# Two pads of 32 bytes between the tile pools of a two-layer decoder trunk

## The chip, the cores and the metric

The kernel runs on one core of one Trainium2 chip. The metric is the device time of one execution in microseconds. The kernel before takes 1494.91 us as the median of three runs (1493.44 to 1496.66). The core has a tensor engine (TensorE, PE in the profile, with PEld for its weight loads), a vector engine (VectorE, DVE), a scalar engine (ScalarE, ACT), GpSimd (POOL) and SyncE (SP), which here issues all DMAs. Two memories matter: SBUF, with 128 partitions in which every tile has a start byte, and PSUM, into which matmuls write.

## The reference

A trunk of two layers over 512 tokens of width 1024, in float32. Each layer is a token mixer, a layer norm, a squared-ReLU MLP of width 4096 with a layer norm, and a gate with a per-layer input p:

```python
for i in range(DEPTH):
    mix = ssd_mixer(x, ...) if i % 2 == 0 else hgrn2_mixer(x, ...)
    h = layer_norm(DEEPNORM_ALPHA * x + mix, ln_g[i, 0], ln_b[i, 0])
    h = layer_norm(DEEPNORM_ALPHA * h + sq_relu_mlp(h, mlp_w1[i], mlp_w2[i]), ln_g[i, 1], ln_b[i, 1])
    x = h + jax.nn.sigmoid(h @ ple_w_gate[i]) * (p[i] @ ple_w_proj[i])
```

Layer 0 mixes with Mamba-2's SSD (an input projection to 5152 columns, a causal convolution, 32 heads in chunks of 128 tokens, an output projection from 2048), layer 1 with HGRN2 (a projection to 4096 columns, 8 heads, an output projection from 1024).

## The kernel before

All projections are made with numbers split in two. A weight unit of 128 x 1024 is loaded by SyncE into a tile `raw`, ScalarE casts it to float32r as the high part `whi` (L104), and VectorE subtracts to get the low part `wlo` (L106). Activations are split in the same way into tiles of the pool `b8`, through the class `Split`, whose `h` and `l` return slices of the high and the low part. A product is then three matmuls that accumulate into one bank of PSUM, high by high, high by low and low by high, which the helper `mm3` issues:

```python
def mm3(out, sh, sl, mh, ml, start, stop):
    nc.tensor.matmul(out, sh, mh, start=start, stop=False)   # L110
    nc.tensor.matmul(out, sh, ml, start=False, stop=False)   # L111
    nc.tensor.matmul(out, sl, mh, start=False, stop=stop)    # L112
```

The first operand (`sh`, `sl`) is loaded into the array as weights, a slice of 128 x 128; the second (`mh`, `ml`) is streamed, 512 or 256 columns at a time. In the profile a matmul reads `out<-streamed,weights`. Every matmul has a weight load of its own, which starts with the matmul before it.

There are three uses of `mm3`:

- `project` and the Strassen products load `whi` and `wlo` as weights and stream the activations: `pj<-b,whi`, `pj<-b,whi`, `pj<-b,wlo` for L110, L111 and L112.
- `out_part`, the gate and the HGRN values load the activations and stream the weights: `pj<-whi,b`, `pj<-wlo,b`, `pj<-whi,b`. In the gate `py<-whi,a` and its like use the split p, `p_s`, in two tiles of the pool `w4`.
- `strassen` makes most pairs of hidden tiles of the MLP with seven products of blocks in place of eight. Four of its blocks are sums; three of these lie in tiles `S`, high part and low part side by side, the fourth in `b8`. `pj<-S,whi`, `pj<-S,whi` and `pj<-S,wlo` are its products with an `S` block, with 256 columns streamed.

The MLP goes over eight groups of four hidden tiles in the order of the list `ORDER`; the first three pairs of hidden tiles are plain products. Outside of HGRN, where TensorE's order is written out, the framework's scheduler orders each engine's work; it gives the weight units a lead.

Memory in SBUF is taken pool by pool, in the order in which the pools are opened: `consts`, `raws`, `whip`, `wlop`, `b8`, `accp`, `w4`, `sm`, and at last one pool per phase for temporaries (`S`, `z`, `xs`, `cv` and others). A pool's tiles have fixed slots one behind the other, and nearly all of these slots are multiples of 512 bytes long. So a pool's start byte fixes the offset of all its tiles, and all slices that the projections' matmuls take start at multiples of 512 bytes from a tile's start.

Of the kernel before, what the change touches and what calls it, by code (L numbers as in the profile page):

```python
# [15 lines left out]
P = 128  # L16
# [13 lines left out]
# the first pairs of hidden tiles are plain products, the others Strassen's  # L30
PLAIN = 3
ORDER = [(w[0], int(w[1])) for w in "h0 b0 h1 o0 h2 o1 h3 o2 h4 o3 h5 o4 h6 o5 h7 o6 o7".split()]
# HGRN: the projections in their order, and how much of them goes between the steps of two heads
# [9 lines left out]
def trunk(ctx: ExitStack, tc, a):  # L43
# [4 lines left out]
    whip = pool("whip", 5)  # L48
    wlop = pool("wlop", 5)
    b8 = pool("b8", 9)  # L50
# [24 lines left out]
    def begin(name):  # L75
        """the pool of temporaries of a phase, in place of the phase before's"""
        if phase:
            phase[1].__exit__(None, None, None)
            phase.clear()
        phase.append(tc.tile_pool(name=name, bufs=1, reuse_waits="tile"))  # L80
        phase.append(phase[0].__enter__())
        phase.reverse()
        phase.append(bufs[name])
# [13 lines left out]
    # ---------------------------------------------------------------- weights  # L97
# [16 lines left out]
    class Split:  # L114
        """[128, n, 512] as high and low parts, in slots of four rows each."""
# [11 lines left out]
    def project(src, xs, ps, m=P, tok=slice(0, T)):  # L127
        """ps[m, tok] = W[:, tile].T @ x.T for a weight unit of eight row tiles."""
        hi, lo = src
        for k in range(8):  # L130
            c = slice(k * m, (k + 1) * m)
            mm3(ps[:m, tok], hi[:, c], lo[:, c], xs.h(k, tok), xs.l(k, tok), k == 0, k == 7)

    # ---------------------------------------------------------------- constants
# [35 lines left out]
    # ---------------------------------------------------------------- layer norm and friends  # L170
# [7 lines left out]
    def layer_norm(c, gb):  # L178
        """acc[:, c] = LN(acc[:, c])"""
        src = acc[:, c, :]  # L180
        st = mk(sm, [P, 2, 6], "lnst")
        for h in range(2):
            nc.vector.bn_stats(st[:, h, :], src[:, h * 512 : (h + 1) * 512])
        mv = mk(sm, [P, 2], "lnmv")
        nc.vector.bn_aggr(mv, st.rearrange("p a b -> p (a b)"))
        sd = mk(sm, [P, 1], "lnsd")
        nc.scalar.activation(sd, mv[:, 1:2], AF.Sqrt, bias=eps)
        rs = mk(sm, [P, 1], "lnrs")
        nc.vector.reciprocal(rs, sd)
        nc.vector.scalar_tensor_tensor(src, src, mv[:, 0:1], gb[0], ALU.subtract, ALU.mult)  # L190
        nc.vector.scalar_tensor_tensor(src, src, rs, gb[1], ALU.mult, ALU.add)

    def transpose_split(src, dst, c, keep=None):
        """dst[:, k, chunk c] = src[tokens, k-th 128 features].T, split; unsplit in keep"""
        sl = slice(c * P, (c + 1) * P)
        for q in range(2):
            pt = bank(pst, "pt")
            for j in range(4):
                k = 4 * q + j
                nc.tensor.transpose(pt[:, j * P : (j + 1) * P], src[:, k * P : (k + 1) * P], ident)  # L200
            v = pt.rearrange("p (j t) -> p j t", j=4)
            h = dst.hi[q][:, :, sl]
            nc.scalar.copy(h, v)
            nc.vector.tensor_sub(dst.lo[q][:, :, sl], v, f32(h))
            if keep is not None:
                nc.scalar.copy(keep[q][:, :, sl], v)

    def out_part(units, n, xs, c, h, first, scale):
        """acc[:, c, half h] += x[:, chunk c].T @ W over n row tiles, each token's row by scale if given;
        acc holds alpha * residual (or the residual, if first)"""  # L210
        sl = slice(c * P, (c + 1) * P)
        ps = bank(psj, "pj")
        for k in range(n):
            hi, lo = units[k // 2]
            ks = slice((k % 2) * 512, (k % 2 + 1) * 512)
            mm3(ps, xs.h(k, sl), xs.l(k, sl), hi[:, ks], lo[:, ks], k == 0, k == n - 1)
        d = acc[:, c, h * 512 : (h + 1) * 512]
        if scale is not None:
            nc.vector.scalar_tensor_tensor(d, ps, scale[:, c : c + 1], d, ALU.mult, ALU.add)
        elif first:  # L220
            nc.vector.scalar_tensor_tensor(d, d, ALPHA, ps, ALU.mult, ALU.add)
        else:
            nc.vector.tensor_add(d, ps, d)  # L223

    def out_project(w, xs, first, after=None, scale=None):
        """w: the four units of four row tiles, by halves of the columns; after(c): what follows the last of chunk c"""
        if after is not None:
            units = [unit(w[i]) for i in range(4)]
            for c in range(NCH):
                for h in range(2):  # L230
                    out_part(units[2 * h : 2 * h + 2], 4, xs, c, h, first, scale)
                after(c)
        else:
            for h in range(2):
                units = [unit(w[2 * h + i]) for i in range(2)]
                for c in range(NCH):
                    out_part(units, 4, xs, c, h, first, scale)

    def norm(i):
        """the norm's result, transposed and split, and what makes its chunk c"""  # L240
        gb = ln_params(i)
        h_s = Split(8)
        keep = [mk(b8, [P, 4, T], "b8") for _ in range(2)] if i % 2 == 0 else None

        def chunk(c):
            layer_norm(c, gb)
            transpose_split(acc[:, c, :], h_s, c, keep)

        return h_s, chunk, keep

    # Winograd's form of Strassen's product: seven products of blocks for eight. The blocks of h.T are
    # [token half][k half], those of the weights [k half][output tile].
    def block_sums(h_s, ht):
        """the four plain and four summed blocks of h.T, as (high, low) of a row tile k"""
# [28 lines left out]
    def weight_sums(src1, src2):  # L283
        """the seven blocks of two weight units: B11, B21, B22, T1, T2, T3, B21 - T2, as (high, low, column)"""
# [24 lines left out]
    def strassen(blocks, src1, src2, z):  # L309
        """z[:, m] = W[:, tile m].T @ h.T for two weight units"""  # L310
# [34 lines left out]
    def mlp_and_gate(layer, h_s, ht, last):  # L345
        """acc holds the normed h. Returns the next x, transposed and split, with x in acc."""
# [40 lines left out]
        # gate  # L387
# [45 lines left out]
    # ---------------------------------------------------------------- layer 0: SSD  # L433
    # time steps
# [36 lines left out]
    # dt * exp(cs_last - cs)  # L471
# [6 lines left out]
    def dt_tail():  # L478
        # token-major copies: [128 tokens, chunk, head]
# [10 lines left out]
    def conv_silu(ps, i, out):  # L490
        """out = silu(causal conv of ps + bias), channel tile i of the convolved ones"""
        cv = tmp("cv", [P, T])
        nc.scalar.activation(cv, ps, AF.Identity, scale=convw[:, i, 3:4], bias=convb[:, i : i + 1])
        for k in range(3):
            d = 3 - k
            nc.vector.scalar_tensor_tensor(cv[:, d:], ps[:, : T - d], convw[:, i, k : k + 1], cv[:, d:], ALU.mult, ALU.add)
        nc.scalar.activation(out, cv, AF.Silu)
# [44 lines left out]
    def core(j, xs, sz, y, toks, btok, cbm, cm):  # L542
# [3 lines left out]
        # token-major x * dt and x * dt * decay to the chunk's end  # L546
# [11 lines left out]
        # chunk states and their scan  # L558
# [13 lines left out]
        # masked decays times C B  # L572
# [9 lines left out]
        # decay from the chunk's start, on channels  # L582
# [33 lines left out]
    def rms_group(ss):  # L616
        """1 / rms of each token of the group: [128 tokens, chunk]"""
# [52 lines left out]
    # ---------------------------------------------------------------- layer 1: HGRN2  # L670
# [6 lines left out]
    # lower bounds: softmax over the one layer, cumulated, less its first row  # L677
# [11 lines left out]
    # The tensor engine's order is fixed here: the projections of the heads to come fill the waits of a head's scores.  # L689
    def vg(i):  # L690
        """values and output gates of heads 2i and 2i + 1, by tokens: [128, chunk, 256]"""
# [80 lines left out]
    def hcore(h, s, i, hl):  # L772
# [12 lines left out]
        def column_sums(f, n):  # L785
            """the sums over the partitions, on each of them"""
# [8 lines left out]
        # the scores of a token with itself and of an odd one with the token before it  # L795
# [63 lines left out]
        # states  # L859
# [23 lines left out]
        # norm and output gate  # L883
# [5 lines left out]
        ri = mk(sm, [P, NCH], "hri")  # L889
# [51 lines left out]
def _tiles_m(w):  # L941
    """[K, M] -> [M/128, 128, K/128 * 128]: one unit per 128 output channels"""
# [4 lines left out]
def _tiles_g(w):  # L947
    """[K, 1024] -> [K/128, 128, 1024]: per four row tiles, two units for each half of the columns"""
# [5 lines left out]
def _tiles_h(w):  # L954
    """[K, 1024] -> [2 * K/256, 128, 2 * 512]: by halves of the columns, two row tiles each"""
# [5 lines left out]
def _tiles_q(w):  # L961
    """[1024, 1024] -> [4, 2, 128, 4 * 256]: by quarters of the columns, four row tiles each"""
# [4 lines left out]
def _cols(v):  # L967
    """[n * 128] -> [128, n]"""
# [3 lines left out]
def _rows(v):  # L972
    """[K, T] -> [128, K/128, T]"""
# [70 lines left out]
```

## Time and profile before

| | |
|---|---|
| median of three runs | 1494.91 us |
| span of the profiled execution | 1492.3 us (the runs' whole times are listed above; for the profiled one the page gives its span) |
| TensorE busy | 1479.3 us, 8848 matmuls |
| weight loads busy (beside the matmuls) | 1280.9 us, 8848 |
| VectorE busy | 1096.4 us, 1786 instructions |
| ScalarE busy | 711.2 us, 968 instructions |
| GpSimd busy | 0.9 us, 8 instructions |
| DMA | 150.07 MB, 101 GB/s on average |
| time in matmuls of L110, L111, L112 on the chain that ended last | 29%, 28%, 28% of the span |

How to read it: matmuls are pipelined, so the duration of one says little of what it costs in a row of them; the distance between the starts of two matmuls in the timeline does. A group's row gives line, engine, operation, tiles, shape and count, then busy us and mean ns of one, then the engine's idle time ahead of it with what ended it.

### The profile page before, as it was taken

The page shows a single profiled execution, that of the slowest core. Times are in us where ns is not written, and L with a number is a line of the kernel's source. Part 1 is how long each engine was busy: PE and PEld are TensorE (multiplying, and loading weights), DVE is VectorE, ACT ScalarE, POOL GpSimd, SP SyncE. Part 2 cuts the span into 40 slices and gives each one's busy share as a digit, 9 for nine tenths or more (in the row PEclk, how much of TensorE's full clock was granted, in tenths as well). Part 3 has the DMA queues.
Part 4 walks back from the last instruction along what each step waited for, and adds up shares of the span by engine and source line. Part 5 has one row for each costly group of instructions (what it writes and reads, how often), then busy time and mean ns, then how long its engine had stood idle before and what let it go on. Part 6 is the DMA issues. An engine that isn't in the chain of part 4 may idle for free.

```text
span 1492.3 us, 21964 instructions
## 1 busy us (share of the span) xinstructions
PE 1479.3 (99%) x8848; PEld 1280.9 (86%) x8848; DVE 1096.4 (73%) x1786; ACT 711.2 (48%) x968; POOL 0.9 (0%) x8
## 2 busy tenths in 40 slices
PE   8999999999999999999999999999999999999998
PEld 5888888888989999888778998989898999998887
DVE  6998677797886777776844767769787777777673
ACT  5777455563564434444334453543364444444342
POOL 0000000000000000000000000000000000000000
PEclk9999999999999999999999999999999999999999
DMA  6433223332233323244223222222123333324322
GB/s 237 169 102 111 98 100 113 100 113 85 71 99 99 113 82 103 88 139 129 94 71 114 86 66 77 70 72 72 57 72 99 114 113 100 110 79 150 115 71 71
DMA packets 41621, 150.07 MB, mean 101 GB/s; under 512 B 4624, under 2 KB 5136, under 8 KB 41392
## 3 DMA queue, kind: packets, MB, share of 16 engines
q1 hardware_dynamic: 41520, 148.67, 30.1%
q8 instruction: 70, 1.15, 0.3%
q14 instruction: 31, 0.25, 0.1%
HBM read 146.49 MB, written 2.16 MB: 100 GB/s over the span
## 4 chain that ended last, share of the span: by engine, by line
PE 97%; DMA 1%; DVE 1%; ACT 1%; issue 0%; SPq 0%; ACTq 0%; DVEq 0%
PE pj L110 29%; PE pj L111 28%; PE pj L112 28%; PE py L782 1%; PE py L591 1%; PE pt L200 1%; PE pm L561 1%; PE py L596 1%; PE py L792 1%; PE py L827 1%; DMA raw<-in_wg 1%; DVE wlo L106 0%; PE pt L549 0%; PE py L880 0%; PE py L112 0%; PE py L110 0%
## 5 line engine op out<-in xcount | busy, mean ns | idle before, releaser
L110 PE MATMUL pj<-whi,b 128*128 128x512 f32 (+1 forms) x1096 | 401.5, 367 | 0.5 <-ACT z L414 0.5
L111 PE MATMUL pj<-wlo,b 128*128 128x512 f32 (+1 forms) x1096 | 399.3, 364 | 0.5 <-DVE wlo L106 0.5
L112 PE MATMUL pj<-whi,b 128*128 128x512 f32 (+1 forms) x1096 | 399.8, 365 | 0.0
L110 PE MATMUL pj<-b,whi 128*128 128x256 f32 (+1 forms) x1024 | 348.0, 340 | 2.1 <-ACT whi L104 2.1
L112 PE MATMUL pj<-b,wlo 128*128 128x256 f32 (+1 forms) x1024 | 344.2, 336 | 0.0
L111 PE MATMUL pj<-b,whi 128*128 128x256 f32 (+1 forms) x1024 | 343.7, 336 | 0.0
L104 ACT CAST whi<-raw 128x1024 fp32r<-128x1024 f32 x192 | 201.4, 1050 | 229.6 <-PE pj L111 133.4
L106 DVE TENSOR_TENSOR wlo<-raw,whi 128x1024 fp32r<-128x1024 f32 x192 | 233.9, 1220 | 64.4 <-ACT whi L104 62.4
L111 PEld LDWEIGHTS pj<-wlo,b 128*128 128x128 f32 x1096 | 206.8, 189 | 32.2 <-DVE wlo L106 1.0
L110 PEld LDWEIGHTS pj<-whi,b 128*128 128x128 f32 x1096 | 206.6, 189 | 32.3 <-ACT z L414 0.7
L112 PEld LDWEIGHTS pj<-whi,b 128*128 128x128 f32 x1096 | 206.7, 189 | 31.7 <-issue 0.2
L110 PEld LDWEIGHTS pj<-b,whi 128*128 128x128 f32 x1024 | 194.5, 190 | 22.0 <-ACT whi L104 4.7
L112 PEld LDWEIGHTS pj<-b,wlo 128*128 128x128 f32 x1024 | 194.4, 190 | 20.3 <-DVE b L150 1.7
L111 PEld LDWEIGHTS pj<-b,whi 128*128 128x128 f32 x1024 | 194.6, 190 | 18.3 <-issue 1.9
L293 ACT CAST whi<-raw 128x1024 fp32r<-128x1024 f32 (+1 forms) x52 | 43.4, 835 | 136.2 <-PE pj L112 110.4
L223 DVE TENSOR_TENSOR acc<-pj,acc 128x512 f32<-128x512 f32 x120 | 81.6, 686 | 35.0 <-PE pj L112 34.5
L110 PE MATMUL pj<-S,whi 128*128 128x256 f32 x312 | 87.4, 280 | 0.0
L111 PE MATMUL pj<-S,whi 128*128 128x256 f32 x312 | 87.0, 279 | 0.0
L112 PE MATMUL pj<-S,wlo 128*128 128x256 f32 x312 | 87.0, 279 | 0.0
L295 DVE TENSOR_TENSOR wlo<-raw,whi 128x1024 fp32r<-128x1024 f32 (+1 forms) x52 | 49.7, 957 | 35.0 <-ACT whi L293 35.0
L293 ACT CAST whi<-a 128x1024 fp32r<-128x1024 f32 x26 | 27.3, 1050 | 94.8 <-PE pj L111 45.5
L110 PEld LDWEIGHTS pj<-S,whi 128*128 128x128 f32 x312 | 58.7, 188 | 0.0
(217 smaller groups left out, 1810.6 us busy)
## 6 DMA issues: line engine op xcount, KB each, us to landing
raw<-in_w SPq DMA_DIRECT2D x128, 512.0 KB, 3.4
raw<-in_wssd SPq DMA_DIRECT2D x40, 512.0 KB, 3.4
a<-csd SPq DMA_DIRECT2D x16, 512.0 KB, 4.0
raw<-in_wso SPq DMA_DIRECT2D x16, 512.0 KB, 3.3
raw<-in_wg SPq DMA_DIRECT2D x16, 512.0 KB, 3.8
raw<-in_whvg SPq DMA_DIRECT2D x16, 512.0 KB, 3.3
raw<-in_whq SPq DMA_DIRECT2D x16, 512.0 KB, 3.3
raw<-in_who SPq DMA_DIRECT2D x8, 512.0 KB, 3.3
```

The source lines that it names most:

```text
L104: nc.scalar.copy(hi[:, :n], raw[:, :n])
L106: nc.vector.tensor_sub(lo[:, :n], raw[:, :n], f32(hi[:, :n]))
L110: nc.tensor.matmul(out, sh, mh, start=start, stop=False)
L111: nc.tensor.matmul(out, sh, ml, start=False, stop=False)
L112: nc.tensor.matmul(out, sl, mh, start=False, stop=stop)
L200: nc.tensor.transpose(pt[:, j * P : (j + 1) * P], src[:, k * P : (k + 1) * P], ident)
L223: nc.vector.tensor_add(d, ps, d)
L293: nc.scalar.copy(hi[:, :n], f)
L295: nc.vector.tensor_sub(lo[:, :n], f, f32(hi[:, :n]))
L561: nc.tensor.matmul(pst_[:, c * P : (c + 1) * P], btok[:, c, :], xw[:, c].rearrange("p h q -> p (h q)"), start=True, stop=True)
L591: nc.tensor.matmul(yd[64 * r : 64 * r + 64, sl], xdt[:, 2 * c + r, :], m[:, r, sl], start=True, stop=True)
L596: nc.tensor.matmul(yo[:, c * P : (c + 1) * P], pv[:, c - 1].rearrange("p h q -> p (h q)"), cm[:, c * P : (c + 1) * P], start=True, stop=True,)
```

## The change

Two pools, `gap1` and `gap2`, are opened between `whip` and `wlop` and between `wlop` and `b8`. Each holds one tile of 128 x 8 float32, 32 bytes in each partition, which is written once and never read. In the same edit all comments and docstrings are taken out, which moves line numbers (L110 to L112 become L112 to L114).

```diff
     whip = pool("whip", 5)
+    gap1 = pool("gap1", 1)
     wlop = pool("wlop", 5)
+    gap2 = pool("gap2", 1)
     b8 = pool("b8", 9)
...
+    for p_ in (gap1, gap2):
+        nc.gpsimd.memset(mk(p_, [P, 8], "gap"), 0.0)
     begin("ssd")
```

The start bytes in the built programs (the first tile of each pool; the others follow at multiples of 128 bytes):

| tiles | before: byte | modulo 128 | after: byte | modulo 128 |
|---|---|---|---|---|
| raw | 21472 | 96 | 21472 | 96 |
| whi | 33760 | 96 | 33760 | 96 |
| wlo | 54240 | 96 | 54272 | 0 |
| b8 | 74720 | 96 | 74784 | 32 |
| acc | 148448 | 96 | 148512 | 32 |
| a and b of w4 | 164832 | 96 | 164896 | 32 |
| S | 189984 | 32 | 190112 | 32 |
| z, xs, cv, cm and the other temporaries of a phase | from 181792 | 32 | from 181920 | 32 |
| ones_r, in consts | 20832 | 96 | 20832 | 96 |

The instructions of TensorE, VectorE, ScalarE and SyncE stand in the same order before and after, with the same shapes and waits. Only GpSimd has more of them. Its rows before, from the start of the program:

```order
L163 MEMSET cm_136 32x512
L166 MEMSET one_139 128x1
L168 MEMSET ones_s_141 128x64
L164 MEMSET cm_136 32x4
L1040 UNCONDITIONAL_BRANCH
```

and in the changed kernel:

```order
L138 MEMSET gap_97 128x8
L138 MEMSET gap_99 128x8
L167 MEMSET cm_146 32x512
L170 MEMSET one_149 128x1
L172 MEMSET ones_s_151 128x64
L168 MEMSET cm_146 32x4
L1044 UNCONDITIONAL_BRANCH
```

The two memsets of the pads stand ahead of the four that were there.

More of the change, by code (lines that the diff above doesn't have):

```diff
@@ L888, in hcore @@
         nc.scalar.activation(ms, ms, AF.Sqrt, scale=1.0 / P, bias=eps)
-        ri = mk(sm, [P, NCH], "hri")
+        ri = mk(sm, [P, 16], "hri")[:, :NCH]
         nc.vector.reciprocal(ri, ms)
```

## The prediction

> **What bounds the kernel now.** I read the page's busy times first, then its chain, then the waits of TensorE, and last the start times of single matmuls.
>
> ```profile
> span 1492.3 us, 21964 instructions
> PE 1479.3 (99%) x8848; PEld 1280.9 (86%) x8848; DVE 1096.4 (73%) x1786; ACT 711.2 (48%) x968; POOL 0.9 (0%) x8
> PE 97%; DMA 1%; DVE 1%; ACT 1%; issue 0%; SPq 0%; ACTq 0%; DVEq 0%
> core 0: 1492.3 us, clock 0.999
> PE pj L438 <- DMA raw<-in_wdt: 4.1, 1, 4.1
> PE pj L110 <- ACT whi L104: 2.1, 1, 2.1
> ```
>
> TensorE is busy for 99% of the span and holds 97% of the chain that ended last; its two longest waits are 4.1 and 2.1 us, and the granted clock is 0.999. No other engine is near it. So a change that leaves the order of the work alone can act only through the pace at which TensorE takes matmuls. That pace is the distance between the starts of two matmuls, not the duration of one: a matmul lasts 0.39 us in these rows while the next starts 0.23 us after it. The timeline of TensorE shows this (start in us, duration in us, line, tiles):
>
> ```profile
> 467.04 0.28 PE L110 MATMUL pj<-S,whi 128*128 128x256 f32 x1
> ...
> 471.29 0.29 PE L110 MATMUL pj<-b,whi 128*128 128x256 f32 x1
> ...
> 472.01 0.28 PE L110 MATMUL pj<-b,whi 128*128 128x256 f32 x1
> ...
> 475.61 0.40 PE L110 MATMUL pj<-whi,b 128*128 128x512 f32 x1
> ...
> 477.00 0.39 PE L110 MATMUL pj<-whi,b 128*128 128x512 f32 x1
> ...
> 497.40 0.28 PE L110 MATMUL pj<-b,whi 128*128 128x256 f32 x1
> ```
>
> This is one Strassen pair and the output projection after it. From 472.01 to 475.61 there are 30 matmuls of 256 columns: 3.60 us / 30 = 120.0 ns each. From 477.00 to 497.40 there are 90 of 512 columns: 20.40 / 90 = 226.7 ns. The 256 columns more cost 106.7 ns, so a column costs 0.417 ns and each matmul has a fixed part of 120.0 - 106.7 = 13.3 ns, the same at both widths. Each matmul also has a weight load of its own that starts with the matmul before it. The fixed part is what one pays for this overlap, and it is the only sum here that addresses could change.
>
> The 36 matmuls from 467.04 to 471.29 have the same shape but stream S in place of b8: 4.25 / 36 = 118.1 ns, a fixed part of 11.4 ns. In the built program S starts at byte 32 modulo 128, while b8, whi and wlo all start at 96, and every slice taken of them is a multiple of 512 bytes. So S over whi is the one pair in this trace of projection operands that differ modulo 128, and it is 1.9 ns cheaper.
>
> **The change part by part.** It adds two memsets of eight elements on GpSimd. Its eight instructions take 0.9 us in all (the POOL entry above), so 0.1 us each; they hide behind the first load, for which TensorE waits 4.1 us. Without that cover they would cost 0.2 us. Nothing else is issued, and the order on TensorE, VectorE, ScalarE and SyncE is the same instruction for instruction, so no DMA is moved past another. What changes is addresses: wlo goes to 0 modulo 128, b8, acc and the w4 tiles to 32; whi and raw stay at 96, S and the phase's other tiles at 32.
>
> The matmuls concerned, from the groups by shape (L111 and L112 have the counts of L110):
>
> ```profile
> L110 PE MATMUL pj<-whi,b 128*128 128x512 f32 x824 | 323.4, 393 | 0.0
> L110 PE MATMUL pj<-b,whi 128*128 128x512 f32 x480 | 194.2, 405 | 2.1 <-ACT whi L104 2.1
> L110 PE MATMUL pj<-b,whi 128*128 128x256 f32 x544 | 153.7, 283 | 0.0
> L110 PE MATMUL pj<-S,whi 128*128 128x256 f32 x312 | 87.4, 280 | 0.0
> L110 PE MATMUL pj<-whi,b 128*128 128x256 f32 x272 | 78.1, 287 | 0.5 <-ACT z L414 0.5
> L110 PE MATMUL py<-whi,a 128*128 128x512 f32 x32 | 12.7, 398 | 0.0
> ```
>
> The name before the comma is streamed, the one behind it is loaded as weights. I pair each streamed operand with the weights that load beside it, those of the next matmul.
>
> A. b8 streamed while whi loads: L110 and L112 of the projections and Strassen products, 2 x (480 + 544) = 2048. The offsets become 32 against 96, exactly those of S over whi, so they take its price: 2048 x 1.9 ns = 3.9 us less.
>
> B. whi streamed while b8 (or the p_s tile) loads: L110 and L112 of the projections back to tokens, 2 x (824 + 272 + 32) = 2256. The distance is again 64 bytes with the roles exchanged, which no row shows. Bounds: the fixed part can't go below zero (13.3 ns less each); upward I use the loss in the slower rival below. The nearest row is S: 1.9 ns, 4.3 us less.
>
> C. The L111 matmuls, where the low part meets wlo at 32 bytes' distance: 1024 + 1128 = 2152, and 312 with S, which leave a distance of 64 for one of 32. No row shows this distance. The bounds are those of B; I take S's price for the 2152, as the nearest row, and nothing for the 312: 4.1 us less.
>
> The sum is 3.9 + 4.3 + 4.1 = 12.3 us.
>
> Some single-precision matmuls move the other way, from a distance of 64 to none, since the w4 tiles a and b join cm, btok and xdt at 32:
>
> ```profile
> L591 PE MATMUL py<-b,xdt 128*64 128x128 f32 x256 | 22.0, 284 | 0.0
> L880 PE MATMUL py<-a,cm 128*128 128x128 f32 x64 | 11.0, 274 | 0.0
> L869 PE MATMUL pm<-a,btok 128*128 128x128 f32 x48 | 6.8, 278 | 0.5 <-DVE pv L873 0.5
> ```
>
> At 1.9 ns more for all 368 that is 0.7 us, and nothing at the other bound; I take 0.3.
>
> Could the other engines feel the addresses? Two groups of VectorE and one row of the table by stretches (busy us of PE, PEld, DVE, ACT in turn):
>
> ```profile
> L106 DVE TENSOR_TENSOR wlo<-raw,whi 128x1024 fp32r<-128x1024 f32 x192 | 233.9, 1220 | 64.4 <-ACT whi L104 62.4
> L374 DVE TENSOR_TENSOR b<-z,b 128x1024 fp32r<-128x1024 f32 x32 | 39.1, 1222 | 13.8 <-ACT b L373 13.8
> 30.00:120.00 90.00, 90.00 (x484) 73.49 (x483) 83.58 (x168) 69.24 (x88) 0.00 (x0) 1.00 0.41 135
> ```
>
> L106 works on tiles that all start at 96, L374 on z at 32 with b8 at 96, and they take 1220 and 1222 ns. So VectorE's cost stays. Its fullest stretch is 30 to 120 us, with 83.58 of 90 us busy while TensorE is busy for all 90: even if VectorE became the bound there, all 484 matmuls' gain at 1.9 ns is 0.9 us. Elsewhere a faster TensorE only asks for weights about 1% sooner, and no wait for weights longer than 2.1 us is listed.
>
> So 12.3 - 0.3 = 12.0 us off the span, 1480.3 us. The median of the runs, 1494.9 us, lies 2.6 us above the profiled span; with that kept, 1482.9, which I round to **1483 us**.
>
> **The rivals.**
>
> *A distance of 32 bytes is much better than 64.* For it speaks that the S pair, which shares its offset modulo 64 with b8, recovers only 1.9 of 13.3 ns, so most of the fixed part may be a conflict that remains at 64. Against it, nothing shows that the rest depends on addresses at all. If C's fixed part halves to 6.7 ns: 2152 x 6.6 + 312 x 4.7 = 15.7 us, with A and B 23.9, so 1492.3 - 23.6 + 2.6 = 1471 us. If B halves too, 2256 x 4.7 = 10.6 us more: 1461. If both vanish, (2152 + 2256) x 13.3 + 312 x 11.4 = 62.2 us, with A 66.1: about 1429, the far end.
>
> *Addresses don't matter, and S is cheaper for another reason.* For it:
>
> ```profile
> 798.00 0.28 PE L110 MATMUL pj<-whi,b 128*128 128x256 f32 x1
> ...
> 798.71 0.28 PE L110 MATMUL pj<-whi,b 128*128 128x256 f32 x1
> ```
>
> These six matmuls stream whi over b8, both at 96, and take 0.71 / 6 = 118.3 ns, as S does. So the pace of one pair of offsets is not one number. Against it, S keeps 118 over all its 36 and the equal offsets keep 120.0 over 30 within the same chain. Then the time stays at 1495 us. The Trainium skill, "TensorE: Matmul & The Clock Gate", section "Step-by-step: what each phase is for", takes this side: TensorE reads its streamed operand and its weights through two independent ports, so that loading the next weights takes nothing from the running matmul. The trace agrees only in part, since 120.0 and 118.1 ns differ with nothing but the tile exchanged. The same page's section "Back-to-back issue gap" gives columns/2.4 + 2.5 ns for a warm stream; here 226.7 ns stand against its 215.8, and if padding reached that figure everywhere, an estimate from the page would be 6768 x 10.8 ns = 73 us less.
>
> *Equal offsets keep the long stream in step, and unequal ones lose it: slower.* From 475.61 to 477.00 above, the first six matmuls of 512 columns take 1.39 / 6 = 231.7 ns, and only then does the stream settle at 226.7. At 256 columns it is the settled stream that is slower (120.0 against 118.3). This looks like two readers that fall into a rhythm, good at 512 columns and bad at 256, and S may be a stream that never settles. If the pads prevent the rhythm, the 3 x (824 + 480 + 32) = 4008 matmuls of 512 columns lose up to 5.0 ns each, 20.0 us, and the 3 x (544 + 272) = 2448 of 256 gain 1.9, 4.7 us: 1492.3 + 15.3 + 2.6 = 1510 us; with half of them unsettled already, 1500. It decides as soon as the loss at 512 columns is over 1.2 ns a matmul (4.7 us / 4008). Against it, S shows no loss, but only at 256 columns.
>
> **How the numbers follow.** My forecast, S's price spread over A to C (1475 to 1490 us), has 0.43; the better distance of 32 0.23; no effect 0.14; the lost rhythm 0.20. So faster is 0.43 + 0.23 = 0.66, within 0.2% (3 us, about what a measurement of this kernel can tell from no change) 0.14, slower 0.20. The range must reach into both outer rivals: down to 1442, which is past the halved fixed parts and leaves the vanished ones out (some 0.07), and up to 1503, about the middle of the slower rival (some 0.10).
>
> **What would show it.** Right: in the changed trace (the three matmul lines are then 112 to 114) b8 over whi at 256 columns steps by 118 ns and 512 columns by 225, while S stays at 118. Step A is wrong if b8 stays at 120 with S's offsets; then the difference isn't the offset. C goes the rival's way if every third step, the one that loads or streams wlo, is short by more than 4 ns. The lost rhythm would show as steps of 229 to 236 ns through the whole output projections. The prediction is wrong outright if VectorE's 1220 ns at L106 moves, or if TensorE gains waits that it doesn't have now.

## The result and the profile after

The changed kernel takes 1509.59 us (median, 1508.93 to 1509.83); the kernel before 1495.79 us over four runs, three of them those given above (1493.44 to 1497.12). The ratio is 1.0093, with a 95% interval of 1.0079 to 1.0106: slower by 0.9%, outside the predicted range, and at the time worked out for the third rival (1510 us).

The page of the changed kernel, with the rows that answer to those shown of before:

```profile
span 1507.7 us, 21966 instructions
PE 1494.1 (99%) x8848; PEld 1277.4 (85%) x8848; DVE 1097.7 (73%) x1786; ACT 710.8 (47%) x968; POOL 1.0 (0%) x10
PE 97%; DMA 1%; DVE 1%; ACT 1%; issue 0%; SPq 0%; ACTq 0%; DVEq 0%
L108 DVE TENSOR_TENSOR wlo<-raw,whi 128x1024 fp32r<-128x1024 f32 x192 | 234.1, 1221 | 66.2 <-ACT whi L106 64.9
```

The span grew by 15.4 us (1492.3 to 1507.7) and TensorE's busy time by 14.8 us, over the same 8848 matmuls; its listed waits grew by 0.7 us in all (8.7 to 9.4). VectorE's subtraction stays at 1221 ns (1220 before), and GpSimd's two memsets added 0.1 us beside other work. So nearly all of the time went into TensorE's own pace. The groups of the projections' first matmul, by shape, say at which width (busy us and mean ns behind the first bar):

```profile
L112 PE MATMUL pj<-whi,b 128*128 128x512 f32 x824 | 327.6, 398 | 0.0
L112 PE MATMUL pj<-b,whi 128*128 128x512 f32 x480 | 195.8, 408 | 2.1 <-ACT whi L106 2.1
L112 PE MATMUL pj<-b,whi 128*128 128x256 f32 x544 | 151.2, 279 | 0.0
```

At 512 columns the busy time rose (323.4 to 327.6, 194.2 to 195.8), at 256 it fell (153.7 to 151.2), and the wait for `whi` is 2.1 us as before. The steps between starts show the price, in the timeline of TensorE at the place that the prediction used (start, duration, line, tiles):

```profile
482.29 0.40 PE L112 MATMUL pj<-whi,b 128*128 128x512 f32 x1
482.52 0.40 PE L113 MATMUL pj<-wlo,b 128*128 128x512 f32 x1
482.76 0.39 PE L114 MATMUL pj<-whi,b 128*128 128x512 f32 x1
...
504.69 0.28 PE L112 MATMUL pj<-b,whi 128*128 128x256 f32 x1
...
506.10 0.28 PE L112 MATMUL pj<-S,whi 128*128 128x256 f32 x1
...
510.33 0.28 PE L112 MATMUL pj<-b,whi 128*128 128x256 f32 x1
```

The output projection from 482.29 to 504.69 has 96 matmuls of 512 columns: 22.40 / 96 = 233.3 ns, where the settled stream before took 226.7. Behind it 12 matmuls of 256 columns that stream b8 take 1.41 / 12 = 117.5 ns (120.0 before), and 36 that stream S 4.23 / 36 = 117.5 (118.1 before).

Added over the whole trace, the distances between the starts of two successive matmuls of one kind and width are (us, worked out from all starts; the last column is e11, below):

| streamed over weights, columns | steps | before | after | e11 |
|---|---|---|---|---|
| whi or wlo over b8, 512 | 2371 | 545.7 | 558.7 | 546.0 |
| b8 over whi or wlo, 512 | 1316 | 310.7 | 315.7 | 311.5 |
| whi or wlo over the split p, 512 | 75 | 17.5 | 17.9 | 17.5 |
| b8 over whi or wlo, 256 | 1604 | 193.4 | 190.0 | 190.7 |
| S over whi or wlo, 256 | 936 | 110.4 | 110.1 | 110.2 |
| whi or wlo over b8, 256 | 780 | 95.2 | 94.7 | 93.1 |

At 512 columns 13.0 + 5.0 + 0.4 = 18.4 us are lost, at 256 columns 3.4 + 0.3 + 0.5 = 4.2 us are won: 14.2 of the 15.4 us. Each row holds all three matmuls of `mm3`, so steps A and B of the prediction share their rows with step C, which has the middle one.

### The profile page after: what moved, and what is told of

Same layout as the page of the kernel before. It is cut to its first block, busy times and chain, and to the rows that moved or that the text cites. A ratio compares the mean times of both kernels' runs of the same rounds, so it can differ in the third digit from the quotient of the medians.

```text
span 1507.7 us, 21966 instructions
## 1 busy us (share of the span) xinstructions
PE 1494.1 (99%) x8848; PEld 1277.4 (85%) x8848; DVE 1097.7 (73%) x1786; ACT 710.8 (47%) x968; POOL 1.0 (0%) x10
## 4 chain that ended last, share of the span: by engine, by line
PE 97%; DMA 1%; DVE 1%; ACT 1%; issue 0%; SPq 0%; ACTq 0%; DVEq 0%
PE pj L112 29%; PE pj L113 29%; PE pj L114 28%; PE py L786 1%; PE py L595 1%; PE pt L204 1%; PE pm L565 1%; PE py L600 1%; PE py L796 1%; PE py L831 1%; DMA raw<-in_wg 1%; DVE wlo L108 0%; PE pt L553 0%; PE py L884 0%; PE py L113 0%; PE py L112 0%
## 5 line engine op out<-in xcount | busy, mean ns | idle before, releaser
L112 PE MATMUL pj<-whi,b 128*128 128x512 f32 (+1 forms) x1096 | 405.6, 371 | 0.5 <-ACT z L418 0.5
L113 PE MATMUL pj<-wlo,b 128*128 128x512 f32 (+1 forms) x1096 | 404.4, 369 | 0.5 <-DVE wlo L108 0.5
L114 PE MATMUL pj<-whi,b 128*128 128x512 f32 (+1 forms) x1096 | 401.0, 366 | 0.0
L112 PE MATMUL pj<-b,whi 128*128 128x256 f32 (+1 forms) x1024 | 347.0, 339 | 2.1 <-ACT whi L106 2.1
L114 PE MATMUL pj<-b,wlo 128*128 128x256 f32 (+1 forms) x1024 | 344.5, 336 | 0.0
L108 DVE TENSOR_TENSOR wlo<-raw,whi 128x1024 fp32r<-128x1024 f32 x192 | 234.1, 1221 | 66.2 <-ACT whi L106 64.9
L112 PEld LDWEIGHTS pj<-whi,b 128*128 128x128 f32 x1096 | 205.9, 188 | 38.0 <-ACT z L418 0.7
L114 PEld LDWEIGHTS pj<-whi,b 128*128 128x128 f32 x1096 | 206.3, 188 | 36.5 <-issue 0.2
L112 PEld LDWEIGHTS pj<-b,whi 128*128 128x128 f32 x1024 | 193.1, 189 | 24.3 <-ACT whi L106 3.9
L114 PEld LDWEIGHTS pj<-b,wlo 128*128 128x128 f32 x1024 | 192.2, 188 | 21.6 <-DVE b L154 1.7
L112 PE MATMUL pj<-S,whi 128*128 128x256 f32 x312 | 87.6, 281 | 0.0
L114 PE MATMUL pj<-S,wlo 128*128 128x256 f32 x312 | 87.4, 280 | 0.0
L112 PEld LDWEIGHTS pj<-S,whi 128*128 128x128 f32 x312 | 58.6, 188 | 0.0
```

The lines of the kernel that those rows point to most:

```text
L108: nc.vector.tensor_sub(lo[:, :n], raw[:, :n], f32(hi[:, :n]))
```

## The experiments

Three theories stood after the result. The first: the step depends only on the distance in bytes between the streamed operand and the weights that load beside it, and equal starts are the best case at 512 columns and a bad one at 256. The second: what decides is where a tile lies, not a distance. The third: the steps come from the traffic of other engines on SBUF, which the pads shift. From here on a distance is the start of the streamed tile less the start of the weights; e5 and e7 will show that it counts modulo 256, and outside of the scan it is given so. In the cuts of code "(the trunk)" and what stands behind `#` are notes of this text.

**e1: the pairs alone.** Only TensorE works, in triples like those of `mm3`, with 48 measured matmuls for each pair of starts; the trunk is left out.

```diff
-    (the trunk)
+    for width in (512, 256):
+        for name, hi, lo, x in CASES:     # bytes added to the starts of whi, wlo and the streamed tile
...
+            for w, s, first in ((wh, xh, True), (wh, xl, False), (wl, xh, False)):
+                nc.tensor.matmul(ps, w, s, start=first and k == first_k, stop=w is wl and k == last_k)
```

> Leaves out the whole trunk: only matmuls like those of mm3 (high by high, high by low, low by high), 12 to lead in and 48 measured for each set of start offsets, with 512 and then 256 columns streamed, no other engine or DMA at work. The weights start at 0 modulo 128, the streamed tile 0 to 112 bytes further; 'shifted' has all at 32, 'pads' has high, low and streamed at 0, 32 and 64 as in the changed kernel. Theory 1 (the pace follows from the offset between the streamed operand and the weights that load beside it, and equal offsets let a 512-column stream settle): 'equal' and 'shifted' step by 226.7 ns at 512 columns and 120.0 at 256; 'pads' by 233 and 118; 'sixtyfour' by 118 at 256. Theory 2 (absolute place counts, not the difference): 'shifted' differs from 'equal'. Theory 3 (the addresses act through other engines' or DMA's accesses to SBUF): all sets step alike, within 1 ns.

The timeline of TensorE has one row for each block of 48, and the "turn" that follows it marks its end; 512 columns first, then 256:

```profile
165.33 11.05 PE L75 MATMUL shifted<-x,w 128*128 128x512 f32 x48
176.22 0.60 PE L67 MATMUL turn<-ident,raw 128*128 128x128 f32 x4
...
179.43 11.27 PE L75 MATMUL pads<-x,w 128*128 128x512 f32 x48
190.53 0.60 PE L67 MATMUL turn<-ident,raw 128*128 128x128 f32 x4
...
193.73 11.04 PE L75 MATMUL equalagain<-x,w 128*128 128x512 f32 x48
204.62 0.60 PE L67 MATMUL turn<-ident,raw 128*128 128x128 f32 x4
```

```profile
282.08 5.92 PE L75 MATMUL shifted<-x,w 128*128 128x256 f32 x48
287.85 0.60 PE L67 MATMUL turn<-ident,raw 128*128 128x128 f32 x4
...
289.69 5.82 PE L75 MATMUL pads<-x,w 128*128 128x256 f32 x48
295.35 0.60 PE L67 MATMUL turn<-ident,raw 128*128 128x128 f32 x4
```

At 512 columns equal starts take 10.89 / 48 = 226.9 ns, as do equal starts that all lie 32 bytes further ("shifted"), and the pads' starts 11.10 / 48 = 231.3 (I had expected 233). These are the pads' distances for b8 streamed over `whi` and `wlo`, 64 and 32; the other direction is not in this run. At 256 columns "shifted" takes 5.77 / 48 = 120.2 and the pads 5.66 / 48 = 117.9. With no other engine at work and both signs present, the third theory falls, and "shifted" speaks against the second.

**e2, e3, e4: parts of the change in the whole kernel.** e2 was meant to move `wlo` alone, by 32 bytes: its two pads put `wlo` at byte 54272 and b8, with all behind it, at 74848, 128 bytes further than before, which was taken for no change. In e3 b8 and all behind it move by 64, `whi` and `wlo` stay together; in e4 all of raw, `whi`, `wlo`, b8 and the rest move by 32 together.

```diff
 e2
     whip = pool("whip", 5)
+    gap1 = pool("gap1", 1)               # 32 bytes
     wlop = pool("wlop", 5)
+    gap2 = pool("gap2", 1)               # 96 bytes
     b8 = pool("b8", 9)
 e3
     wlop = pool("wlop", 5)
+    gap1 = pool("gap1", 1)               # 64 bytes
     b8 = pool("b8", 9)
 e4
+    gap1 = pool("gap1", 1)               # 32 bytes, ahead of the pool raws
```

> Pads of 32 and 96 bytes: only wlo moves (to 0 modulo 128), b8, acc and S keep their offsets against whi. Two of three matmuls then run with equal offsets, as before, the third (L111's kind) at 32 bytes' distance. Theory 1 (any unequal pair takes the 512-column stream out of its rhythm): slower than before by 5 to 15 us, 1500 to 1510, and the steps at 512 columns 229 to 236 ns. Rival (only the distance of 32 costs, and it costs the changed kernel's whole loss): as slow as the changed kernel or slower, 1509 to 1515, the third step alone long. Rival (the distance of 64 costs, 32 does not): 1495 or less.

> One pad of 64 bytes ahead of b8: all weights stay at 96, the activations go to 32, so that every projection's pair is 64 bytes apart; S goes to 96 and becomes equal to whi. Theory 1: 512 columns step by 229 to 236 ns, b8 over whi at 256 by 118, S by 120; 1500 to 1512 us. Rival (64 gains at both widths as my forecast had it, only 32 loses): b8 at 256 columns 118 ns and 512 columns 225 ns, 1480 to 1487 us.

> One pad of 32 bytes ahead of raws: all weights and activations move together, whi, wlo, b8 and acc to 0 modulo 128, S to 64, still 64 from whi. Theory 1 (only differences count): as before, 1494 to 1496 us, 226.7 and 120.0 ns. Theory 2 (absolute place counts): another time by more than 3 us.

The kernel before, beside them: 1495.36 us. e2 took 1500.45 us, ratio 1.0035 (1.0022 to 1.0048); e3 1504.28, 1.0058 (1.0043 to 1.0073); e4 1494.87, 0.9998 (0.9988 to 1.0007). In e2 the timeline has the output projection between these rows:

```profile
480.36 0.39 PE L112 MATMUL pj<-whi,b 128*128 128x512 f32 x1
480.59 0.39 PE L113 MATMUL pj<-wlo,b 128*128 128x512 f32 x1
...
502.33 0.28 PE L112 MATMUL pj<-b,whi 128*128 128x256 f32 x1
```

96 matmuls take 21.97 / 96 = 228.9 ns. The time, at the lower edge of what the first theory gave, looks like the price of a distance of 32 in one matmul of three, but it isn't: modulo 256 b8 has moved by 128, so `whi` and b8 are 128 apart in e2, `wlo` and b8 160 or 96, and no projection pair is equal. e2 does show that a step isn't priced by its own pair alone. In this projection the steps that start with L112 and with L114 both stream `whi` at a distance of 128, and they take 230.8 and 226.0 ns.

e4 has a pad, its memset and a new start for every tile but those of `consts`, and keeps every sum of the table above to 0.7 us, so none of these costs anything: the second theory falls too, and only distances are left.

e3 has every projection pair at two distances, b8 over the weights at 64 and the weights over b8 at 192, and none at 32. Its output projection takes 22.40 / 96 = 233.3 ns, as in the changed kernel:

```profile
478.98 0.39 PE L111 MATMUL pj<-whi,b 128*128 128x512 f32 x1
...
501.38 0.28 PE L111 MATMUL pj<-b,whi 128*128 128x256 f32 x1
```

Its sums, added as in the table above, change by +14.0 us for `whi` or `wlo` over b8 at 512 columns and +0.4 over the split p, by +1.8 for b8 over `whi` or `wlo`, and at 256 columns by -3.2 (b8) and -4.0 (`whi` or `wlo` over b8). The values of HGRN, which stream `whi` over b8 at 256 columns, step in e3 from 832.80 to 835.86 us through 27 matmuls, 113.3 ns:

```profile
832.80 0.28 PE L111 MATMUL pj<-whi,b 128*128 128x256 f32 x1
...
835.86 0.28 PE L111 MATMUL pj<-whi,b 128*128 128x256 f32 x1
```

So a distance can be worth 6.7 ns at 256 columns. A miss in e3 was S: at a distance of 128 its sum was 111.1 us, against 110.4 before, though I had expected the price of equal starts.

**e5: a scan of distances.** The kernel of e1 with `whi` and `wlo` together and 38 distances of the streamed tile.

```diff
-    ("pads", 0, 32, 64),
...
+WORDS = {
+    "a": 0, "b": 4, "c": 8, "d": 12, "e": 16, "f": 20, "g": 24, "h": 28, "i": 32, "j": 36, "k": 40, "l": 44, "m": 48,
...
+    "zd": 256, "ze": 368, "zf": 512,
+}
+CASES = [("d" + w, 0, 0, at) for w, at in WORDS.items()]
```

> Leaves out the whole trunk, as e1_pairs_alone: 38 distances of the streamed operand from the weights (0 to 124 bytes in steps of 4, then 128, 192, 240, 256, 368 and 512), 36 measured matmuls each, with 512 and with 256 columns. If the pace is a function of the distance modulo 128 alone: 128, 256 and 512 repeat 0 (226.9 and 120.0 ns), 192 repeats 64 (229 and 117.7), 240 and 368 repeat 112 (231 and 113.3). If a larger period counts, some of these differ by more than 2 ns. If equal offsets are the best place for 512 columns, no distance comes below 226 ns there; at 256 columns 112 should not be the lowest by chance: its neighbours 108 to 120 should lie within 4 ns of 113.

Six blocks at 512 columns (start, duration of 36 matmuls) at distances of 0, 64, 128, 192, 256 and 512 bytes:

```profile
21.52 8.32 PE L67 MATMUL da<-x,w 128*128 128x512 f32 x36
...
207.19 8.41 PE L67 MATMUL dq<-x,w 128*128 128x512 f32 x36
...
393.48 8.53 PE L67 MATMUL dza<-x,w 128*128 128x512 f32 x36
...
405.09 8.56 PE L67 MATMUL dzb<-x,w 128*128 128x512 f32 x36
...
428.44 8.33 PE L67 MATMUL dzd<-x,w 128*128 128x512 f32 x36
...
451.35 8.33 PE L67 MATMUL dzf<-x,w 128*128 128x512 f32 x36
```

A block lasts 35 steps and the last matmul, so 0.21 us more for 128 than for 0 are 6 ns a step. The mean steps of the settled blocks, worked out from all starts:

| distance, bytes | 0 | 16 | 32 | 64 | 112 | 128 | 192 | 240 | 256 | 368 | 512 |
|---|---|---|---|---|---|---|---|---|---|---|---|
| 512 columns, ns | 226.7 | 231.7* | 233.3 | 228.9 | 231.1 | 232.5 | 233.3 | 236.8 | 226.7 | 231.1 | 226.7 |
| 256 columns, ns | 120.0 | 113.3 | 116.7* | 117.8 | 113.3 | 120.0 | 113.3 | 117.2 | 120.0 | 113.3 | 120.0 |

(* e1 has the same.) At 512 columns no distance beats 0, and the dearest took 240.0 ns (20, 68, 100 and 116 bytes). At 256 columns 0 is among the dear ones, and the good places are narrow: 112 took 113.3 ns, its neighbours 108, 116 and 120 about 120 to 122, though I had expected them within 4 ns of 113. The row repeats after 256 bytes: 256 and 512 equal 0 and 368 equals 112 at both widths, while 128 does not equal 0 at 512 columns, nor 192 equal 64. I saw this last part only after e6. Single readings have to be taken with care, since one distance can have more than one pace (e10): 16 bytes at 256 columns took 113.3 ns here and 116.7 in e1.

**e6: Strassen's weights 16 bytes further.** Only the 256-column products are to change. The slots of `whi` and `wlo` grow to hold the shift, here to 4224 bytes.

```diff
+SHIFT = 4
...
-            hi = mk(whip, [P, 1024], "whi", F32R)
+            hi = mk(whip, [P, 1056], "whi", F32R)
...
-                nc.scalar.copy(hi[:, :n], f)
+                nc.scalar.copy(hi[:, SHIFT : SHIFT + n], f)
```

> The kernel before, with the split weights of the Strassen products 16 bytes further in their slots and a pad of 64 bytes that puts S at 96 modulo 128: at 256 columns b8 and S are then streamed 112 bytes past the weights, at 512 columns all stays equal. Theory 1 (the pace follows from the distance, as in the bare matmuls): b8 steps by 113.3 ns in place of 120.0 (1632 matmuls, 10.9 us) and S by 113.3 in place of 117.9 (936 matmuls, 4.3 us), so 1478 to 1483 us. Rival (in the kernel the other engines' accesses or the changes between groups set the pace, or the entry of each group after the switch eats it): 1490 to 1496 us.

It took 1503.82 us against 1495.66, ratio 1.0054 (1.004 to 1.0068), slower than both ranges: a miss. Slots of 4224 = 16 x 256 + 128 bytes put every second weight tile 128 bytes off. With a period of 128 that would have been harmless; the 512-column steps came out mixed, between 226 and 236 ns.

**e7: a period of 128 or of 256.** b8 and all behind it move by 128 bytes, which leaves every offset modulo 128 as it was.

```diff
     wlop = pool("wlop", 5)
+    gap = pool("gap", 1)                 # 128 bytes
     b8 = pool("b8", 9)
```

> One pad of 128 bytes ahead of b8: modulo 128 every offset is as in the kernel before, modulo 256 the activations are 128 from the weights, and S goes from 64 to 192 past whi. Period 128, as the change's words have it: no change, 1494 to 1497 us. Period 256, as the bare matmuls showed (128 apart: 232.5 and 120 ns; 192 apart: 113.3 ns at 256 columns): the some 2770 matmuls of 512 columns that settle at 226.7 ns before lose 5.8 ns each, 16 us, and the 936 with S gain 4.5 ns each, 4 us: 1505 to 1510 us.

1505.52 us against 1495.02, ratio 1.0071 (1.0058 to 1.0085), as expected for 256: with the scan, where 256, 368 and 512 repeat 0, 112 and 0, the period is 256. e2 has the starts of e7 in all pools but `wlo`, which in e2 lies 32 bytes further, and took 1500.45 us: the place of `wlo` alone is worth some 5 us. S lies at a distance of 192 here, and the timeline has 36 of its matmuls and then 48 with b8, at 128:

```profile
462.35 0.29 PE L111 MATMUL pj<-S,whi 128*128 128x256 f32 x1
...
466.46 0.28 PE L111 MATMUL pj<-b,whi 128*128 128x256 f32 x1
...
472.16 0.28 PE L111 MATMUL pj<-S,whi 128*128 128x256 f32 x1
```

S takes 4.11 / 36 = 114.2 ns and b8 5.70 / 48 = 118.8.

**e8 and e9: a distance of 112 for the 256-column products alone.** Slots of 17 x 256 bytes keep all tiles of one pool equal modulo 256; Strassen's weights begin 144 bytes into their slots, which puts b8 and S 112 bytes on from them. e9 also moves the weights of the HGRN values by 192 bytes.

```diff
+SLOT = 1024 + 64
+SHIFT = 36
...
-            hi = mk(whip, [P, 1024], "whi", F32R)
+            hi = mk(whip, [P, SLOT], "whi", F32R)[:, s : s + 1024]
...
+    nc.gpsimd.memset(mk(gap, [P, 48], "gap"), 0.0)      # a pad of 192 bytes before sm
...
-                hi = mk(whip, [P, 1024], "whi", F32R)
+                hi = mk(whip, [P, SLOT], "whi", F32R)[:, SHIFT : SHIFT + 1024]
 e9
-            units = [unit(a["whvg"][4 * i + 2 * which + j]) for j in range(2)]
+            units = [unit(a["whvg"][4 * i + 2 * which + j], s=48) for j in range(2)]
```

> The kernel before with slots of 4352 bytes for whi and wlo, so that all slots keep their offset modulo 256, the Strassen products' weights 144 bytes into their slots and a pad of 192 bytes for S: b8 and S are then streamed 112 bytes past the weights modulo 256 at 256 columns, and all pairs at 512 columns stay equal. Theory 1 with a period of 256: b8 and S at 256 columns step by 113.3 ns (10.9 and 4.2 us less), 512 columns by 226.7: 1478 to 1483 us. Rival (the settled pace doesn't hold in the kernel's short groups): 1490 to 1496 us.

> As e8_strassen_112, and the weights of the HGRN values and gates 192 bytes into their slots, so that they are streamed 192 bytes past b8 modulo 256 at 256 columns. Theory 1: another 3 to 5 us less than e8_strassen_112 (e3_distance_64 had these steps at 113 to 114 ns by the same distance), 1473 to 1479 us. Rival: as e8_strassen_112 within 2 us, since those matmuls are interleaved with others and settle seldom.

Beside a kernel before of 1495.02 us, e8 took 1497.09, ratio 1.0014 (1.0005 to 1.0023), and e9 1495.28, 1.0001 (0.9992 to 1.001). Theory 1 missed in both; the rival had e9 right and e8 too low by 1 us. The 512-column sums went back to 546.2 and 311.3 us, as expected, but S and b8 did not run at 113.3 ns. In e8:

```profile
457.38 0.28 PE L113 MATMUL pj<-S,whi 128*128 128x256 f32 x1
...
461.69 0.28 PE L113 MATMUL pj<-b,whi 128*128 128x256 f32 x1
```

4.31 / 36 = 119.7 ns, where the scan had 113.3 at the same distance. e9's values fell from 95.3 to 93.0 us in their sum.

**e10: what a stream is entered from.** Bare matmuls again: 36 measured ones behind 24 of another kind, "wide" (512 columns, distance 0), "narrow" (256, distance 0) or "off" (256, distance 64).

```diff
+LEADS = {"wide": (512, 0), "narrow": (256, 0), "off": (256, 64)}
...
+            for what, steps, cols, x in (("lead", 8, lead_width, lead_at), (name, 12, width, at)):
```

> Leaves out the whole trunk, as e1_pairs_alone: 36 measured matmuls, entered from 24 matmuls of another kind: 512 columns with equal offsets (wide), 256 columns with equal offsets (narrow), 256 columns 64 bytes apart (off). If the pace is a function of the distance modulo 256 alone, every kind of entry gives the same steady steps: 226.7, 228.9 and 233.3 ns at 512 columns for 0, 64 and 192; 120, 113 to 117, 117.8, 113.3 and 113.3 ns at 256 columns for 0, 16, 64, 112 and 192. If a distance has more than one steady rhythm and the entry picks one, 112 shows 120 ns after at least one kind of entry (as in e8_strassen_112) and 113.3 after another; 192, which kept 113.3 in the kernel of e7_act_128, should hold it after all three.

Two blocks at a distance of 192 and 256 columns, each with the "turn" behind it (names longer than a row are cut at the left):

```profile
238.59 4.40 PE L65 MATMUL inetytwo_after_wide<-x,w 128*128 128x256 f32 x36
242.83 0.60 PE L57 MATMUL turn<-ident,raw 128*128 128x128 f32 x4
...
246.14 4.26 PE L65 MATMUL etytwo_after_narrow<-x,w 128*128 128x256 f32 x36
250.24 0.60 PE L57 MATMUL turn<-ident,raw 128*128 128x128 f32 x4
```

The same 36 matmuls take 4.24 / 36 = 117.8 ns after wide ones and 4.10 / 36 = 113.9 after narrow ones, and each keeps its rhythm to the end of the block. Likewise a distance of 64 at 512 columns settled at 233.3 ns after narrow ones and at 228.9 after the other two. Equal starts had one rhythm after all three: 226.7 and 120.0. I had expected 192 at 256 columns to hold 113.3 after all three, and it did not. The distance that I had expected to change, 112, took 113.3 after all three. Why the whole kernel runs it at 120 stays open.

**e11: a distance of 192 in place of 112.** e9 with another shift.

```diff
-SHIFT = 36
+SHIFT = 16
```

> As e9_and_values, with the Strassen products' weights 64 bytes into their slots, so that b8 and S are streamed 192 bytes past them modulo 256. Theory 1 (192 has its fast rhythm in the kernel too, as S had in e7_act_128): b8 120.0 to 113.3 ns (1632 matmuls, 10.9 us), S 117.9 to 113.3 (936, 4.3 us), the values' matmuls a further 2 us: 1476 to 1481 us. Rival (the entry from equal 512-column matmuls picks the slow rhythm, as it did at 112): 1493 to 1498 us.

1490.26 us against 1495.37, ratio 0.9963 (0.9949 to 0.9976): faster than both kernels by more than the noise, and between the ranges of the theory and of the rival. The timeline has 48 matmuls with b8 and, ahead of them, 36 with S:

```profile
458.06 0.28 PE L113 MATMUL pj<-S,whi 128*128 128x256 f32 x1
...
462.30 0.28 PE L113 MATMUL pj<-b,whi 128*128 128x256 f32 x1
...
467.95 0.28 PE L113 MATMUL pj<-S,whi 128*128 128x256 f32 x1
```

S takes 4.24 / 36 = 117.8 ns and b8 5.65 / 48 = 117.7: the pace of the slower of the two rhythms that e10 showed for 192, the one entered from 512 columns. In the kernel too the group shown follows on an output projection of 512 columns; that this is the reason was not tested in place. In the table above e11 has the 256-column gains (2.7, 0.2 and 2.1 us) and hardly any of the 512-column loss (0.3 + 0.8 us).

## Why the prediction was wrong, point by point

**Right.** TensorE is the bound, and its pace is nearly all that changed: order, VectorE's 1220 ns and the granted clock stayed, the waits grew by 0.7 us, and a pad with its memset cost nothing (e4: 1494.87 us against 1495.36). That offsets matter, against the rival that they don't, holds from both sides: e4 moves nearly all addresses and no time, e1 shows the effect with nothing else at work. At 256 columns step A was right, and for its reason: b8 over `whi` came to S's distance of 64, was to fall to S's 118.1 ns and steps by 117.5 here, 3.4 us over all its matmuls. That S stayed at its price (118.1, then 117.5) was luck: modulo 256 its distance went from 64 to 192 for `whi` and 160 for `wlo`, and with both at 192 S ran at 114.2 ns in e7.

**The step that failed: S's price put on 512 columns.** Steps A to C charged -1.9 ns to every matmul that got an unequal offset, 2 x 480 of 512 columns in A, 2 x (824 + 32) in B, and their share in C. S had been measured only at 256 columns, and I carried it over because I took the fixed part of 13.3 ns as one cost, the same at both widths. It isn't one cost. At 512 columns equal starts are the cheapest of all the distances that the scan tried, so an unequal offset could only lose there: 18.4 us over the 3762 steps of the table, 4.9 ns each, where I had -1.9. The sign was wrong, and not only the size.

**Within it, step B: "the distance is again 64 bytes with the roles exchanged".** That holds modulo 128. The period is 256 (e5, e7): modulo 256 `whi` starts at 224 and b8 at 32 after the change, so b8 over whi is at 64 and whi over b8 at 192. In the scan these cost 228.9 and 233.3 ns at 512 columns. e3 has these two distances alone, and prices them in the kernel: +14.0 and +0.4 us in the rows of B, which had -1.9 ns a matmul, and +1.8 us in the row of A. The output projection steps by 233.3 ns there and in the changed kernel, +6.6 ns. So B is the dearest part of the loss.

**Step C** had no row for a distance of 32 and took S's price. In e1 a distance of 32 by itself takes 233.3 ns at 512 columns, 6.6 more than equal starts, and 116.7 at 256, 3.3 less. In the kernel the changed version beside e3 shows it best: the two differ only in `wlo`, by 32 bytes, and in S and the other temporaries, by 64. The changed kernel takes 1509.59 us, e3 1504.28. Added as in the table, the sums grow from e3 by 3.2 us for b8 over `whi` or `wlo` at 512 columns and by 3.6 for `whi` or `wlo` over b8 at 256, and shrink by 1.1 for `whi` or `wlo` over b8 at 512 and by 0.9 for S. So the move of `wlo` cost some 5 us on top of A and B, where C had 4.1 us less, and the largest part of it is at S's own width: the values of HGRN, whose steps have a mean of 116.9 ns in e3, have one of 121.6 in the changed kernel.

**The rivals.** "32 bytes is much better" falls: at 512 columns 32 takes 233.3 ns in e1.

The second rival, that addresses don't matter, falls with e1. The Trainium skill, "TensorE: Matmul & The Clock Gate", section "Step-by-step: what each phase is for", which the prediction cites for it, has weights and streamed operand come in through independent ports, so that a load takes no SBUF read bandwidth from the running matmul. The runs here don't bear this out for the pace: with nothing but the start of the streamed tile changed, e5 has steps from 226.7 to 240.0 ns at 512 columns. (The formula that gives 215.8 ns, cited in the same place, is given in its section for a matmul by itself and not, as the prediction has it, for a stream; the lowest steady pace that any run here shows at 512 columns is 226.7.)

The third rival had place and price: it put 20.0 us on 512 columns and -4.7 on 256, and 18.4 and -4.2 were measured; its time, 1510 us, is the result, and its marker, steps of 229 to 236 ns through whole output projections, is what the timeline shows. That it met the time to half a microsecond is partly luck: its 5.0 ns was meant as the most that a matmul could lose, and the mean of 4.9 is made up of 5.5 ns for the weights over b8 and 3.8 for b8 over the weights. Its picture was off too. The unequal stream does settle, but into a slower rhythm of three steps (700 ns for three in the changed kernel, 680 before). The evidence it rested on, six unsettled matmuls at 231.7 ns ahead of a settled 226.7, was worth more than the 0.20 I gave it: it was the only row with a second pace at 512 columns, where 4008 of the matmuls are.

**Open.** Which structure of SBUF or of TensorE has the period of 256 bytes was not found; the runs show the dependence, not its mechanism, and give no rule for the pace of a triple whose three distances differ (e2). Nor is it settled why a distance of 112 runs at 120 ns in the kernel and at 113.3 alone.

## What to carry to other kernels

Where every matmul has its own weight load, as the float32r matmuls here, and TensorE bounds the kernel, compare start bytes of streamed tiles and weights modulo 256, and keep them equal for 512-column streams; a price found at one width says nothing of another. Keep slot sizes at multiples of 256, so that a pool's tiles share an offset. A scan of bare matmuls ranks the offsets in one run, but which rhythm a kernel then falls into depends on what runs ahead, so measure it in place.

## What the runs showed of the hardware that was not expected

- The step of back-to-back float32r matmuls with a weight load each depends on the distance between the streamed operand and the weights, with a period of 256 bytes: 226.7 to 240.0 ns at 512 columns, and from 113.3 ns to 123.3 (4 bytes, e1) at 256.
- The order of the distances differs between the widths: 0 is the best at 512 columns (226.7) and among the worst at 256 (120.0 against 113.3).
- One distance can have more than one steady rhythm, and what ran ahead picks it: 192 at 256 columns held 117.8 ns after 512-column matmuls and 113.3 after 256-column ones (e10).
